# A hybrid encoder layer on one core: most of the values' products made in two row tiles of 64 contraction rows, each with its own bank, summed at the evacuation

## The chip, the core and the metric

The kernel runs on one NeuronCore of a Trainium2 chip. TensorE (PE) multiplies: it loads a stationary operand of up to 128x128 (a weight load, PEld in the profile) and streams a moving operand of up to 512 columns past it; the result goes to a bank of PSUM, of which there are eight, each 128 x 512 fp32. VectorE (DVE) and ScalarE (ACT) read PSUM and work on SBUF, GpSimd (POOL) works on SBUF alone, and SyncE (SP) issues most of the transfers between HBM and SBUF. Each engine works through its own queue in order; semaphores order the engines among each other.

The metric is device time in microseconds of one launch, the median of the runs. Lower is better.

## The reference

One layer is run (DEPTH is 1): an RMS norm, one projection to queries, keys, values and a gate, neighbourhood attention on a 32 x 64 grid of tokens, a SiLU gate, the output projection with its residual, and a final RMS norm. 2048 tokens, width 1024, 16 heads of 64.

```python
def neighbourhood_mixer(h, w_in, rpb):
    B, S, _ = h.shape
    proj = h @ w_in
    q, k, v, gate = jnp.split(proj, 4, axis=-1)
    heads = lambda a: a.reshape(B, S, N_HEADS, HEAD_DIM)
    o = neighbourhood_attention(heads(q), heads(k), heads(v), rpb)
    return o.reshape(B, S, D_INNER), gate
...
        h = rmsnorm(x, g)
...
            o, gate = neighbourhood_mixer(h, w_in, rpb)
...
        x = x + (o * jax.nn.silu(gate)) @ w_out
    return rmsnorm(x, norm_f)
```

The change touches the part of `h @ w_in` that makes the values v.

## The kernel before

All large products are made in rounded fp32 (the type F32R). To keep the precision, an operand is split into a high half `h` (ACT rounds it with a copy) and a low half `l` (DVE subtracts the high half from the operand). A product of two operands is three matmuls into one bank: high x high, high x low, low x high.

The contraction over the width of 1024 has eight steps `k` of 128 rows. Tokens are split into four blocks of 512, and a block into four tiles of 128.

*Values.* `values_of(X1, u, ts, ks)` (lines 549 to 560) makes the values of the token tiles `ts` for the unit `u` (512 columns of values; two units) over the steps `ks`. The stationary operand is 128 rows (the step) by 128 tokens of x, the moving one 128 rows by the 512 columns of the weights: an output of 128 tokens by 512 columns in one bank, named "pv". With eight steps and three matmuls each, a tile takes 24 matmuls. With 16 tiles and two units there are 768. After each, `due(1)` advances a count by which delayed work (stores above all) is issued.

`evac_v(u, t, p)` (line 389) takes a finished bank: ACT copies it with a scale to an SBUF tile `v`, and eight counts later SP stores that tile to a DRAM buffer `vd`. The weights of the values are split by `split_v` (line 532) into `W[u, b]`, a pair of tiles of two steps each, b = 0 to 3; ACT makes the high halves (line 539) and DVE the low ones (line 542). The four pairs fill the eight buffers of the pool `wp`, so the second unit's pair b can be written only once the first unit's pair b has been used for the last time.

*The rest of the projections.* Queries, keys and gate of tokens 0 to 1023 (stage one), and in part those of tokens 1024 to 2047 (stage two), are made by `seven_products` (line 402), with seven products in place of eight, line 435. Those left over are made during the attention (lines 379 to 383).

*Order.* Each engine's queue follows the order of the program, which is written out by hand. In stage one, unit 0's tiles come first: 0 to 3 together, 4 and 5, 6 and 7. Then come unit 1's tiles one by one through `tile_v` (line 757), in the order 4, 5, 6, 7, 0, 1, 2, 3, with other work handed in after each: the evacuation of the tile before, forms of x for the seven products, and twice `spread_rstd` (line 226), two full matmuls (lines 229 and 230) into a bank of its own that ACT copies (line 235). In stage two, `pair(u, ts, *do)` (line 831) goes through the four blocks of weights b, for each makes the products of the tiles `ts`, and then issues the piece `do[b]`. Unit 0's tiles 8 to 15 are made two at a time, unit 1's one at a time:

```python
        pair(0, (8, 9), both(w(0, 3), lambda: spread_rstd(3)), both(lw(1, 0), block("B12", x12, 0, 1)), block("B12", x12, 2, 3),
             block("B22", x22, 0, 1))
        pair(0, (10, 11), both(v(0, 8, 9), block("B22", x22, 2, 3)), t123(0), t123(1), lw(1, 1))
        pair(0, (12, 13), v(0, 10, 11), t123(2), t123(3), both(t4(0, 1, 2, 3), lw(1, 2)))
        pair(0, (14, 15), both(v(0, 12, 13), w(1, 0)), both(w(1, 1), lw(1, 3)), w(1, 2), w(1, 3))
```

Here `w(u, b)` splits a block of weights, `lw` loads one, `v` evacuates tiles, `block` scales and splits a block of x (lines 513, 517, 518), and `t123` and `t4` form differences of x on DVE (lines 862 to 870). Just before, the last seven products of stage one are evacuated: DVE adds (line 453), GpSimd scales (line 455), and for the gate ACT makes a tanh (line 359) and DVE a product (line 360).

*Banks.* Every bank comes from one pool of eight, in turn (`bank`, line 117): a new one waits until whoever read the bank eight allocations before has finished.

*Attention.* The scores (line 1027) and the transposes (line 1112) are plain fp32 and use row tiles already: the two heads of a pair lie on partitions 0 to 63 and 64 to 127 and write to separate banks. The products with the values (line 1134) use two column tiles of 64. A matmul of plain fp32 stands in the trace as two records, a transpose as one.

Of the kernel before, what the change touches and what calls it, by code (L numbers as in the profile page):

```python
# [14 lines left out]
AF = mybir.ActivationFunctionType  # L15
OP = mybir.AluOpType
# [5 lines left out]
NK = D // 128  # L22
# [48 lines left out]
def build(ctx, tc, x, xr, xt, wg, rpb, last, w_out, n0, nf, masks, out):  # L71
    nc = tc.nc
# [44 lines left out]
    def bank(n, name):  # L117
        return banks.tile([128, n], F32, name=name, tag="bank")
# [12 lines left out]
    rth = one.tile([128, 8], F32, name="rth")  # L131
# [125 lines left out]
    for n, (k, j, ph, c) in enumerate(halves):  # L257
        a = (KINDS[k] + j, ph)
# [66 lines left out]
    def store(key, lag, f):  # L325
        n = len(later)
        while n and later[n - 1][0] > clock[0] + lag:
            n -= 1
        later.insert(n, (clock[0] + lag, key, f))

    def due(n):
        clock[0] += n
        while later and later[0][0] <= clock[0]:
            later.pop(0)[2]()
# [53 lines left out]

    def evac_v(u, t, p):
        v = ev([128, 512], F32, "v")  # L390
        nc.scalar.activation(v, p, AF.Copy, scale=rth[:, t:t + 1] if t < 8 else 0.5)
        dst = vd[u].rearrange("h n d -> n h d")[t * 128:t * 128 + 128]
        written.add(("v", u, t))
        store(("v", u, t), 8, lambda: nc.sync.dma_start(dst, v.rearrange("p (h d) -> p h d", h=4)))
# [128 lines left out]
    VR, W = {}, {}  # L523
# [23 lines left out]
    ps = {}  # L547

    def values_of(X1, u, ts, ks):
        for t in ts:  # L550
            if ks[0] == 0:
                ps[t] = bank(512, "pv")
        for k in ks:
            x = X1["B%d%d" % (k // 4 + 1, ts[0] // 4 % 2 + 1)][k % 4]
            h, l = W[u, k // 2][0][:, k % 2], W[u, k // 2][1][:, k % 2]
            for m, (a, b) in enumerate(((x[0], h), (x[0], l), (x[1], h))):
                for t in ts:
                    o = slice(t % 4 * 128, t % 4 * 128 + 128)
                    nc.tensor.matmul(ps[t], a[:, o], b, start=k == 0 and m == 0, stop=k == NK - 1 and m == 2)  # L559
                    due(1)  # L560

    def place_of(slot_):
        return slot_[0]([128, slot_[1]], F32R, "t")[:, :512] if isinstance(slot_, tuple) else slot_

    X2 = {}
# [4 lines left out]
    def stage_one():  # L570
        us = [("k", j) for j in range(4)] + [(k, j) for j in range(4) for k in "qg"]
        X1 = {f: [(xs([128, 512], F32R, "h"), xs([128, 512], F32R, "l")) for _ in range(4)]
              for f in ("B12", "B11", "B21", "B22")}
# [120 lines left out]
        for k in range(NK):  # L694
            if k == 0:
                for h in range(2):
                    if h == 0:
                        split_v(0, 1, 0, (0,), nc.vector)
                    split_to(*(t[:, parts_[h]] for t in X1["B11"][0]), land["x11"][0][:, parts_[h]], gain("x11", 0))
                    if h == 0:  # L700
                        split_v(0, 0, 0, (0,), fresh=False)
                    values_of(X1, 0, (2 * h, 2 * h + 1), (0,))
                continue
            elif k == 1:
                split_v(0, 0, 0, (1,))
                split_v(0, 1, 0, (1,))
            elif k in (2, 3):
                split_v(0, 0, 1, (k - 2,))
                split_v(0, 1, 1, (k - 2,))
            elif k % 2 == 0:  # L710
                split_v(0, 0, k // 2)
                split_v(0, 1, k // 2)
            f = "x%d1" % (k // 4 + 1)
            split("B" + f[1:], land[f][k % 4], k % 4, f)
            values_of(X1, 0, (0, 1, 2, 3), (k,))
# [4 lines left out]
        for a, b in ((0, 0), (1, 0), (0, 1), (1, 1)):  # L720
            load_v0(1, a, b)
        values_of(X1, 0, (4, 5), range(4))
        for k in range(4):
            split("B22", land["x22"][k], k, "x22")
# [4 lines left out]
        for t in range(4):  # L729
            evac_v(0, t, ps[t])  # L730
# [4 lines left out]
        for b in range(4):  # L735
            values_of(X1, 0, (6, 7), (2 * b, 2 * b + 1))
            if b == 0:
                split_v(1, 0, 0)
                split_v(1, 1, 0)
                square_rows(*halves_of(1)[4:])  # L740
                stats(1)
                for t in (4, 5):
                    evac_v(0, t, ps[t])
            else:
                split_v(1, 0, b)
                split_v(1, 1, b)
        for k in range(4):
            y = ev([128, 512], F32, "y")
            a, b, c = land["x11"][k], land["x12"][k], land["x22"][k]
# [4 lines left out]
        for t in (6, 7):  # L754
            evac_v(0, t, ps[t])

        def tile_v(t, *do):
            values_of(X1, 1, (t,), range(NK))
            for f in do:
                f()  # L760

# [5 lines left out]
        def some(f, x, *ks):  # L767
            return lambda: [split(f, land[x][k], k) for k in ks]
# [4 lines left out]
        def t1(*ks):  # L773
            return lambda: [split("T1", land["x12"][k], k, "x11") for k in ks]

        v = lambda t: lambda: evac_v(1, t, ps[t])
        tile_v(4, some("T2", "x11", 0, 1, 2, 3))
        tile_v(5, v(4), t4, slot(-9), some("T3", "x22", 0, 1))
        tile_v(6, v(5), some("T3", "x22", 2, 3), slot(-8, -7))
        tile_v(7, v(6), lambda: diagonal(0), some("T4", "x21", 0), slot(-6))  # L780
        tile_v(0, v(7), lambda: spread_rstd(0), some("T4", "x21", 1), lambda: diagonal(1))
        tile_v(1, v(0), lambda: spread_rstd(1), t1(0, 1, 2))
        tile_v(2, v(1), t1(3), some("T4", "x21", 2, 3))
        values_of(X1, 1, (3,), (0, 1))
        v(2)()
        ahead(-5)
        values_of(X1, 1, (3,), (2, 3))
        ahead(-4)
        ahead(-3)
        values_of(X1, 1, (3,), (4, 5))  # L790
        ahead(-2)
        values_of(X1, 1, (3,), (6, 7))
        ahead(-1)
        v(3)()
        run()
# [2 lines left out]
    def stage_two():  # L798
# [30 lines left out]
        ahead, run = seven_products(units_two, 2, X2, also)  # L829

        def pair(u, ts, *do):
            for b in range(4):
                values_of(X2, u, ts, (2 * b, 2 * b + 1))
                if b < len(do):
                    do[b]()

        def both(*fs):
            return lambda: [f() for f in fs]
# [42 lines left out]
        def t1(*ks):  # L881
            def g():
# [3 lines left out]
            return g  # L886
# [6 lines that stand above are left out]
        pair(1, (12,), v(0, 14, 15), form("T2", x11, 0), form("T2", x11, 1))  # L893
# [530 lines left out]

    pair_steps = range(10, 24, 2)
    stage_one()
    stage_two()
    attending[0] = True
    for m in range(cycles + 1):
        a = amount[m] - 8  # L1430
# [111 lines left out]
```

## Time and profile before

| | |
|---|---|
| Time, median of 3 runs | 1057.04 us (1056.35 to 1057.21) |
| Span of the profiled execution | 1054.4 us |
| Busy: PE / PEld | 1046.1 us (99%) / 858.8 us (81%) |
| Busy: DVE / ACT / POOL | 696.7 us (66%) / 537.2 us (51%) / 252.0 us (24%) |
| Records of PE matmuls | 7316 |
| Chain that ended last: line 435 / line 559 | 36% / 17% |

The profile is of one execution, and of that the span from its first to its last instruction is given; its time with what lies around the span is not listed apart. Records are listed as start, duration, engine, line, operation, output<-inputs, tile (rows by columns of the stationary operand for PE) and shape; "x2" means that two records in sequence were merged, and the duration runs to the end of the second. A note in brackets gives the idle time of the engine before the record and what ended it. Groups are listed as shape, count, busy time (overlaps counted once) and mean duration in ns. PE's records overlap, since a matmul ends some time after the next one has started: the pace is read from starts.

### The profile page before, as it was taken

Reading aid. Unit: us, or ns where it says so; the run is one execution under the profiler, and the core shown is the slowest. Engines: PE = TensorE matmul, PEld = TensorE weight load, DVE = VectorE, ACT = ScalarE, POOL = GpSimd, SP = SyncE. Lnnn points to the kernel's source line nnn. Section 1 sums busy time; section 2 is a strip of 40 time slices with the busy share of each in tenths; the row PEclk is TensorE's granted clock in tenths of the full one; section 3 lists DMA queues with packets and bytes.
Section 4 is the critical chain, followed back from the end, with each engine's and each line's share of the span. In section 5 each row is a group of like instructions: output and inputs, shape, how many; then the busy total and the mean of one; then the engine's idle time right before and its main releaser. Section 6 shows DMA issues by size and latency. Waiting matters only on the chain.

```text
span 1054.4 us, 20160 instructions
## 1 busy us (share of the span) xinstructions
PE 1046.1 (99%) x7316; PEld 858.8 (81%) x7316; DVE 696.7 (66%) x1570; ACT 537.2 (51%) x1260; POOL 252.0 (24%) x342
## 2 busy tenths in 40 slices
PE   9999999999999999999999999999999999999997
PEld 7888888887888888888888788888887888888886
DVE  5476667778897625555655766687777886667554
ACT  7645223443444334232332677688787865455422
POOL 0000322312211000000002467666665322112100
PEclk9999999999999999999999999999999999999999
DMA  9634444343635433333236777778777588775352
GB/s 320 219 100 118 132 150 136 120 144 120 187 119 154 121 100 93 116 110 121 90 110 211 219 232 235 219 252 281 243 237 217 184 277 272 245 233 183 120 166 80
DMA packets 120252, 184.19 MB, mean 175 GB/s; under 512 B 10776, under 2 KB 55064, under 8 KB 120152
## 3 DMA queue, kind: packets, MB, share of 16 engines
q1 hardware_dynamic: 119720, 182.50, 55.1%
q8 instruction: 57, 0.93, 0.4%
q10 hardware_dynamic: 432, 0.40, 0.1%
q14 instruction: 43, 0.35, 0.1%
HBM read 132.53 MB, written 50.33 MB: 173 GB/s over the span
## 4 chain that ended last, share of the span: by engine, by line
PE 96%; DVE 2%; issue 1%; ACT 1%; DMA 0%; SPq 0%; DVEq 0%; ACTq 0%
PE pp L435 36%; PE pv L559 17%; PE s L1027 8%; PE o L1134 8%; PE po L1346 6%; PE po L1348 5%; PE po L1350 5%; PE ph L1112 4%; PE pp L381 2%; PE pp L383 2%; PE pp L379 2%; DVE f L418 0%; DVE x L1035 0%; DMA raw<-in_wg_dram 0%; DVE raw L424 0%
## 5 line engine op out<-in xcount | busy, mean ns | idle before, releaser
L435 PE MATMUL pp<-h,f 128*128 128x512 f32 x672 | 217.4, 389 | 0.0
L1041 ACT ACTIVATE x<-x,st 128x360 f32<-128x360 f32 (+5 forms) x256 | 151.1, 592 | 23.0 <-DVE st L1035 23.0
L1055 POOL TENSOR_SCALAR x<-x,st 128x480 f32<-128x480 f32 (+5 forms) x192 | 111.7, 599 | 153.5 <-DVE st L1046 148.6
L435 PEld LDWEIGHTS pp<-h,f 128*128 128x128 f32 x672 | 126.2, 188 | 26.2
L435 PE MATMUL pp<-t,f 128*128 128x512 f32 x558 | 141.7, 389 | 0.1
L435 PE MATMUL pp<-l,f 128*128 128x512 f32 x336 | 130.7, 389 | 0.0
L1035 DVE CUSTOM_DVE_ANT_0 x<-s,em 128x360 f32<-128x360 f32 (+5 forms) x256 | 123.0, 535 | 0.5 <-PE s L1027 0.4
L435 PEld LDWEIGHTS pp<-t,f 128*128 128x128 f32 x558 | 104.7, 188 | 22.2 <-DVE u L448 0.6
L455 POOL TENSOR_TENSOR tmp<-tmp,rb 128x512 f32<-128x512 f32 x36 | 58.4, 1622 | 268.3 <-DVE tmp L453 232.8
L995 POOL TENSOR_TENSOR em<-e,mk 128x264 f32<-128x264 f32 (+3 forms) x64 | 50.8, 825 | 259.8 <-PE pp L435 246.3
L418 DVE TENSOR_TENSOR f<-raw,f 128x512 fp32r<-128x512 f32 x105 | 76.5, 729 | 43.6 <-ACT f L417 43.5
L1346 PE MATMUL po<-woh,gh 128*128 128x512 f32 x252 | 99.8, 396 | 0.1
L1348 PE MATMUL po<-woh,gl 128*128 128x512 f32 x252 | 98.7, 391 | 0.0
L1350 PE MATMUL po<-wol,gh 128*128 128x512 f32 x252 | 98.6, 391 | 0.0
L1027 PE MATMUL s<-kt,q 64*128 64x480 f32 (+5 forms) x512 | 94.6, 487 | 0.0
L1134 PEld LDWEIGHTS o<-pta,vt 120*64 120x64 f32 (+2 forms) x1792 | 80.9, 137 | 13.9 <-DVE st L1035 13.6
L559 PE MATMUL pv<-wh,h 128*128 128x512 f32 x256 | 88.3, 390 | 0.0
L559 PE MATMUL pv<-wl,h 128*128 128x512 f32 x256 | 88.2, 390 | 0.2 <-DVE wl L542 0.2
L559 PE MATMUL pv<-wh,l 128*128 128x512 f32 x256 | 88.2, 389 | 0.0
L1088 DVE COPY pta<-ph 120x512 f32<-120x512 f32 (+5 forms) x96 | 56.9, 639 | 43.5 <-PE ph L1112 43.3
L1134 PE MATMUL o<-pta,vt 120*64 120x128 f32 (+5 forms) x1792 | 85.3, 253 | 0.0
L1027 PEld LDWEIGHTS s<-kt,q 64*128 64x128 f32 x512 | 64.9, 186 | 15.3 <-DVE pta L1088 1.3
(156 smaller groups left out, 1705.3 us busy)
## 6 DMA issues: line engine op xcount, KB each, us to landing
raw<-in_wg_dram SPq DMA_DIRECT2D x124, 256.0 KB, 4.3
row<-in_xr_dram SPq DMA_DIRECT2D x32, 256.0 KB, 4.1
vd<-v SPq DMA_DIRECT2D x32, 256.0 KB, 2.5
sgd<-sg SPq DMA_DIRECT2D x32, 256.0 KB, 2.4
q<-qd SPq DMA_DIRECT2D x32, 256.0 KB, 5.2
sgt<-sgd SPq DMA_DIRECT2D x32, 256.0 KB, 4.9
xr<-in_x_dram SPq DMA_DIRECT2D x32, 256.0 KB, 3.8
ogd<-og SPq DMA_DIRECT2D x32, 256.0 KB, 2.7
```

Of the source, the lines that this page charges most:

```text
L418: nc.vector.tensor_tensor(t[:, 1], src, t[:, 0].bitcast(F32), OP.subtract)
L435: nc.tensor.matmul(B[n, P], t[:, int(m == 2), c], x[k][int(m == 1)], start=P in (1, 6, 5) and k == 0 and m == 0, stop=k == 3 and m == 2, s ...
L455: nc.gpsimd.tensor_tensor(tmp, tmp, rb[c], OP.mult)
L559: nc.tensor.matmul(ps[t], a[:, o], b, start=k == 0 and m == 0, stop=k == NK - 1 and m == 2)
L1027: nc.tensor.matmul(pst[s], qt[a, qs], kt[a, :r1 - r0, c0:c1].rearrange("p r (s c) -> p s r c", c=8), start=True, stop=True)
L1035: nc.vector.tensor_tensor_reduce(X[i, C][s], pst[s], EM[p, ROW_TYPE[T], COL_TYPE[C], s], -1.0, 1e38, OP.add, OP.min, st[:, o:o + 1])
L1041: nc.scalar.activation(X[i, C][s], X[i, C][s], AF.Exp, bias=st[:, o:o + 1], scale=-1.0, accum_out=st[:, 4 + o:5 + o])
L1055: nc.gpsimd.tensor_scalar(X[i, C][s], X[i, C][s], st[:, o:o + 1], 1.0, op0=OP.mult, op1=OP.mult)
L1134: nc.tensor.matmul(to.rearrange("d (h q) -> d h q", q=64) if nq > 64 else to, vt[:k, strip, s * 64:s * 64 + 64], t[:k, h, at:at + 64] if n ...
L1346: nc.tensor.matmul(p, gh, woh[q, j], start=(i == 0), stop=False)
L1348: nc.tensor.matmul(p, gl, woh[q, j], start=False, stop=False)
L1350: nc.tensor.matmul(p, gh, wol[q, j], start=False, stop=(i == NK - 1))
```

## The change

The values' products of unit 1 in stage one and of both units in stage two go through a new function. It takes one token tile at a time, gives it two banks ("pv" and "pw"), and makes every matmul twice: once with rows 0 to 63 of both operands into the first bank, once with rows 64 to 127 into the second. `due(1)` is counted once for both. The evacuation copies the first bank with the scale, as before, and then DVE multiplies the second bank by the same scale and adds it to the tile. The stores take the tile after that.

In stage two a pair of tiles is no longer made block by block together: all four blocks of the first tile come first, then those of the second. The pieces handed in keep their numbers and are spread over both tiles, so that with two tiles a piece follows every second block.

Stage one's unit 0 stays with `values_of`.

```diff
     def evac_v(u, t, p):
         v = ev([128, 512], F32, "v")
-        nc.scalar.activation(v, p, AF.Copy, scale=rth[:, t:t + 1] if t < 8 else 0.5)
+        scale = rth[:, t:t + 1] if t < 8 else 0.5
+        nc.scalar.activation(v, p[0] if isinstance(p, tuple) else p, AF.Copy, scale=scale)
+        if isinstance(p, tuple):
+            nc.vector.scalar_tensor_tensor(v, p[1], scale, v, op0=OP.mult, op1=OP.add)
...
+    def values_halved(X1, u, t, ks):
+        if ks[0] == 0:
+            ps[t] = bank(512, "pv"), bank(512, "pw")
+        o = slice(t % 4 * 128, t % 4 * 128 + 128)
+        for k in ks:
+            x = X1["B%d%d" % (k // 4 + 1, t // 4 % 2 + 1)][k % 4]
+            h, l = W[u, k // 2][0][:, k % 2], W[u, k // 2][1][:, k % 2]
+            for m, (a, b) in enumerate(((x[0], h), (x[0], l), (x[1], h))):
+                for r in range(2):
+                    q = slice(64 * r, 64 * r + 64)
+                    nc.tensor.matmul(ps[t][r], a[q, o], b[q], start=k == 0 and m == 0, stop=k == NK - 1 and m == 2)
+                due(1)
...
         def tile_v(t, *do):
-            values_of(X1, 1, (t,), range(NK))
+            values_halved(X1, 1, t, range(NK))
...
-        values_of(X1, 1, (3,), (0, 1))
+        values_halved(X1, 1, 3, (0, 1))
         v(2)()
         ahead(-5)
-        values_of(X1, 1, (3,), (2, 3))
+        values_halved(X1, 1, 3, (2, 3))
...
         def pair(u, ts, *do):
-            for b in range(4):
-                values_of(X2, u, ts, (2 * b, 2 * b + 1))
-                if b < len(do):
-                    do[b]()
+            for n, t in enumerate(ts):
+                for b in range(4):
+                    values_halved(X2, u, t, (2 * b, 2 * b + 1))
+                    i = (4 * n + b) // len(ts)
+                    if (4 * n + b) % len(ts) == len(ts) - 1 and i < len(do):
+                        do[i]()
```

More of the change, by code (lines that the diff above doesn't have):

```diff
@@ L783, in stage_one @@
         tile_v(2, v(1), t1(3), some("T4", "x21", 2, 3))
-        values_of(X1, 1, (3,), (0, 1))
+        values_halved(X1, 1, 3, (0, 1))
         v(2)()
         ahead(-5)
-        values_of(X1, 1, (3,), (2, 3))
+        values_halved(X1, 1, 3, (2, 3))
         ahead(-4)
         ahead(-3)
-        values_of(X1, 1, (3,), (4, 5))
+        values_halved(X1, 1, 3, (4, 5))
         ahead(-2)
-        values_of(X1, 1, (3,), (6, 7))
+        values_halved(X1, 1, 3, (6, 7))
         ahead(-1)
```

## The prediction

> **What bounds the kernel now.** I read the page first (busy shares, the granted clock, the chain that ended last), then the busy time of each engine over the three stretches of the values' products that the change touches.
>
> ```profile
> span 1054.4 us, 20160 instructions
> PE   9999999999999999999999999999999999999997
> PEclk9999999999999999999999999999999999999999
> PE 96%; DVE 2%; issue 1%; ACT 1%; DMA 0%; SPq 0%; DVEq 0%; ACTq 0%
> core 0: us, PE busy (x) PEld busy (x) DVE busy (x) ACT busy (x) POOL busy (x), PEclk, DMA share, GB/s
> 48.30:93.30 45.00, 45.00 (x199) 37.18 (x198) 31.98 (x56) 25.62 (x45) 0.00 (x0) 1.00 0.37 101
> 323.10:367.40 44.30, 44.30 (x196) 36.63 (x196) 30.68 (x47) 14.80 (x26) 1.77 (x2) 1.00 0.45 124
> 367.40:410.70 43.30, 43.30 (x192) 35.86 (x191) 16.02 (x26) 17.39 (x33) 0.00 (x0) 1.00 0.32 92
> ```
>
> PE is the bound: 96% of the chain, full clock, and in the three stretches busy from edge to edge. So a change of the PE stream counts one for one; what DVE and ACT get counts only where PE must wait for it. How fast PE goes there is the distance between starts, not the length of a record, since records overlap:
>
> ```profile
> 379.67 0.39 PE L559 MATMUL pv<-wl,h 128*128 128x512 f32 x1
> ...
> 381.94 0.39 PE L559 MATMUL pv<-wh,l 128*128 128x512 f32 x1
> 379.90 0.19 PEld L559 LDWEIGHTS pv<-wh,h 128*128 128x128 f32 x1
> ```
>
> Ten steps take 2.27 us: one product of 128x512 every 0.227 us. The weight load of 0.19 us starts with a product (379.90) and is over before the next one starts, so it costs at most the small gap that is left between two streams.
>
> **The products (576 of them).** L559 makes 768 values' products; those of tiles 0 to 7 of unit 0 (192) stay, 8 tiles of unit 1 in stage one (192) and 16 tiles in stage two (384) are halved. Each becomes two, of 64 rows, with the same 512 columns. No work is saved: half the contraction rows stream as many columns. If the two tiles run side by side, a pair takes about what one product took; what a pair really takes no row shows, so I bound it.
>
> ```profile
> L1027 PE MATMUL s<-kt,q 64*128 64x480 f32 x128 | 30.9, 566 | 0.0
> L1134 PE MATMUL o<-pta,vt 120*64 120x128 f32 x512 | 38.9, 276 | 0.0
> L1134 PE MATMUL o<-pta,vt 120*64 120x64 f32 x384 | 21.9, 221 | 0.0
> ```
>
> The two L1134 rows differ by 55 ns over 64 columns: 0.86 ns a column for a pass of plain fp32. At that, the 128 records of the scores (L1027, two row tiles in two banks) would need 128 x 480 x 0.86 = 52.8 us one after the other; they are busy 30.9 us. So row tiles do run side by side here, in plain fp32. If a column of the rounded fp32 takes half as long as a plain one (an assumption), 512 columns stream in 220 ns, and 7 of the 227 ns are gap; the rows are rounded, and with a difference of 54 ns it would be 216 and 11. Lower end: the gap vanishes, 216 to 220 ns a pair, -7 to -11 ns. Upper end: nothing overlaps, 454 ns. Between them: the gap belongs to each tile (its own weights, its own stream) and stays: 227 ns, and some ns for the second start. I take 228, +1 ns a pair, 576 x 1 = +0.6 us, because the gap sits between a tile's own two streams, and a second tile with the same rhythm does not fill it. A higher price without serialising is the widest spacing of two full products in sequence:
>
> ```profile
> 325.88 0.40 PE L229 MATMUL prb<-dgh,onesr 128*128 128x512 f32 x1
> 326.12 0.40 PE L230 MATMUL prb<-dgl,onesr 128*128 128x512 f32 x1
> 326.36 0.63 PE L559 MATMUL pv<-wh,h 128*128 128x512 f32 x2
> ```
>
> 240 ns, +13 ns a pair. [...]
>
> **Changes between full and halved mode.** There are ten: into the halved tiles and out (2 in each stage), and around `spread_rstd` (4 in stage one, 2 in stage two).
>
> ```profile
> 660.64 0.39 PE L379 MATMUL pp<-h,w 128*128 128x512 f32 x1
> 660.96 0.42 PE L1112 MATMUL ph<-ident,x 64*88 64x64 f32 x8
> ```
>
> From a full product to the 64-row tiles 0.32 us pass instead of 0.227: 0.09 us. Taken for each way: +0.9 us (lower end 0.45, if the way back is free).
>
> **The order in stage two.** `pair(0,(8,9))` went through the four blocks of weights with both tiles; now tile 8 takes all four, then tile 9. The work handed in between keeps its place (after 12 products), but tile 8 needs the fourth block after 18 pairs, not after 36 products. Is it there?
>
> ```profile
> 323.15 0.62 PE L559 MATMUL pv<-wh,h 128*128 128x512 f32 x2
> 326.35 1.62 POOL L455 TENSOR_TENSOR tmp<-tmp,rb 128x512 f32<-128x512 f32 x1 [3.09 <-issue]
> 327.99 0.63 ACT L359 ACTIVATE sg<-tmp 128x512 f32<-128x512 f32 x1 [4.07 <-POOL tmp L455]
> 328.53 1.14 ACT L539 ACTIVATE wh<-raw 128x512 fp32r<-128x512 f32 x2
> 329.57 0.58 ACT L235 ACTIVATE rb<-prb 128x512 f32<-128x512 f32 x1
> 329.27 1.28 DVE L542 TENSOR_TENSOR wl<-raw,wh 128x512 fp32r<-128x512 f32 x2
> ```
>
> The two splits of block 3 stand on ACT behind the gate's tanh (L359), which waits for GpSimd: high half at 329.67, low half at 330.55, 6.5 and 7.4 us after the stage's first product at 323.15. Before, PE came there after 36 x 0.227 + 0.7 (spread) = 8.9 us, so nothing waited. Now it comes after 18 x 0.227 + 0.7 + 0.2 (two changes of mode) = 5.0 us: it waits 1.5 to 1.6 us for the high half, makes one pair, and waits another 0.65 us for the low half. **About +2.25 us**, on the path, as nothing else is in PE's queue. ACT's order is not touched, so the wait is not earlier work's doing.
>
> Next comes the bank. A tile takes two of eight banks in turn, `spread_rstd` one: tile 11's second bank is tile 8's first, which ACT frees:
>
> ```profile
> 341.51 0.63 ACT L517 ACTIVATE h<-land 128x512 fp32r<-128x512 f32 x1 [1.42 <-DVE land L513]
> 342.05 1.07 ACT L391 ACTIVATE v<-pv 128x512 f32<-128x512 f32 x2
> 342.53 0.59 ACT L391 ACTIVATE v<-pv 128x512 f32<-128x512 f32 x1
> ```
>
> The first evacuation ends at 342.6, 19.5 us after 323.15. PE comes to tile 11 at 72 x 0.228 + 0.7 + 0.3 + 2.25 = 19.6 us: no more wait. But a faster pair would only wait there: up to tile 11, this stretch cannot gain.
>
> Unit 0's weights are now let go by tile 15 (after 30, 36, 42, 48 pairs of the last pair), not by both tiles at once; unit 1's splits wait for that and are used 18 pairs (4.1 us) later each.
>
> ```profile
> 361.51 1.15 ACT L539 ACTIVATE wh<-raw 128x512 fp32r<-128x512 f32 x2 [1.56 <-PE pv L559]
> 362.17 1.29 DVE L542 TENSOR_TENSOR wl<-raw,wh 128x512 fp32r<-128x512 f32 x2 [1.43 <-ACT wh L539]
> ```
>
> One block takes 362.17 + 1.29 - 361.51 = 1.95 us of the 4.1: hidden, with 2.1 us to spare; later blocks come every 1.36 us and DVE needs 1.29. I cost it at nothing.
>
> **The sum at the evacuation.** 24 more DVE operations with one operand in PSUM.
>
> ```profile
> L448 DVE TENSOR_TENSOR u<-pp,p 128x512 f32<-128x512 f32 x42 | 28.9, 689 | 24.7 <-PE pp L435 24.7
> L391 ACT ACTIVATE v<-pv 128x512 f32<-128x512 f32 x16 | 9.1, 593 | 33.6 <-issue 18.0 <-PE pv L559 15.6
> ```
>
> At 0.69 us (the like of L448) that is 16.5 us of DVE, 5.5 in each of the three stretches, where it is idle 13.0, 13.6 and 27.3 us by the windows above. It covers them; were it full, each would cost 0.69 us. Each now waits on DVE for ACT's copy, and what stands behind it there (block B22's last two, `t123`) moves some 1.4 us per pair of tiles; tile 12 needs B22 only 9 us later. The stores on SP's queue wait for DVE instead of ACT, about 1 us longer, and the weight loads behind them are used over 10 us later. Cost: nothing.
>
> **Sum.** Products +0.6, mode +0.9, late weights +2.25: **+3.8 us**, against the profiled execution a span of 1058.2. That execution is told by its span of 1054.4; the median of the runs is 2.6 us above it, so 1057.0 + 3.8 = **1060.8 us**. Bounds of the unmeasured prices in this case: spacing 227 to 231 and mode 0.45 to 0.9 give +2.7 to +5.5, so 1059.7 to 1062.5.
>
> **Rivals.**
> *The gap closes* (the other side): place, the gap between two streams of the same tile; price g per pair. For it: L1027 shows that tiles overlap. Against it: no row shows a gap filled by the other tile. Only 504 pairs count (72 stand before tile 11's bank), and against them 2.5 us at tile 11 and 7 x 0.09 for mode: 3.1 - 0.504 g. It decides from g = 6.2 ns (220.8 a pair). At 220, -0.4: 1056.6. At 216, -2.4: 1054.6. [...] Faster by over 0.2% (2.1 us; less than that a measurement of this kernel cannot tell from no change) needs 10.3 ns, so about half of this case.
> *The tiles run one after the other*: rounded fp32 may use the array's whole input. For it: 30.9 us over 128 x 480 columns is 0.50 ns a column of both tiles together, no faster than the full product's 227/512 = 0.44; side by side the halves would need 0.22, which no row shows. Against it: plain fp32 overlaps. 576 x 0.227 = +130.8, mode +0.9, no wait for weights: 1188.7. In that case the change does not do what it says.
> *Dearer pairs*: 240 ns. 576 x 13.3 = 7.7, mode 0.9, weights 2.0 (PE comes 0.24 us later): +10.6, 1067.6.
>
> **Chances.** Gap stays (forecast) 0.40, gap closes 0.34, one after the other 0.15, dearer pairs 0.11. Range 1054.6 to 1067.6: it leaves out the serial case and the edges of the two others, a little under 0.2. The likeliest case's own range is 1059.7 to 1062.5. Faster: half of the closing gap, 0.17. Same: its other half and a sliver of the forecast, 0.19. Slower: 0.64.
>
> **What would show it.** The spacing of pairs in the middle of stage two (228 against 220 or less, 240, 454). A wait of PE of about 1.6 and 0.65 us some 5 us after stage two begins, put down to wh and wl. No wait, or a tenth, at tile 11 if pairs take 228; half a microsecond if they are faster. 0.09 us at each change of mode. The sums at 0.69 us, and no PE wait named after them. Wrong it would be if PE waits for a bank in stage one or at tiles 12 to 15, or if DVE's sums push out work that PE needs.

## The result, and the profile after

The changed kernel takes 1061.57 us (four runs, 1060.88 to 1062.33) against 1057.04: a ratio of 1.0046, 95% interval 1.0031 to 1.006. On another chip it took 1060.88 (1059.96 to 1062.12) against 1056.90, ratio 1.0040 (1.0027 to 1.0054). It is slower, by 4 to 4.5 us.

The page of the changed kernel, its span and its chain:

```profile
span 1059.7 us, 21345 instructions
PE 95%; DVE 2%; issue 1%; ACT 1%; POOL 0%; DVEq 0%; ACTq 0%
```

The bound is the same. The span is 5.3 us longer than before, and the time of every run lies 1.8 us above its span. Where the 5.3 us are is read from PE's timeline. Each matmul of line 575 stands twice, first bank (pv) and second bank (pw); columns are start, duration, engine, line.

In the middle of stage two:

```profile
356.48 0.39 PE L575 MATMUL pv<-wh,h 64*128 64x512 f32 x1
356.48 0.39 PE L575 MATMUL pw<-wh,h 64*128 64x512 f32 x1
...
357.16 0.39 PE L575 MATMUL pv<-wh,h 64*128 64x512 f32 x1
```

The two tiles of a pair start within the same hundredth of a microsecond, and three pairs take 0.68 us: 0.227 us a pair, what one full product took. The two tiles run fully side by side, and nothing is won or lost by it.

Around `spread_rstd` in stage two:

```profile
327.07 0.39 PE L575 MATMUL pv<-wh,l 64*128 64x512 f32 x1
...
327.39 0.50 PE L229 MATMUL prb<-dgh,onesr 128*128 128x512 f32 x1
327.73 0.39 PE L230 MATMUL prb<-dgl,onesr 128*128 128x512 f32 x1
328.04 0.49 PE L575 MATMUL pv<-wh,h 64*128 64x512 f32 x1
...
328.38 0.39 PE L575 MATMUL pv<-wl,h 64*128 64x512 f32 x1
...
328.61 0.39 PE L575 MATMUL pv<-wh,l 64*128 64x512 f32 x1
```

Five steps take 1.54 us; at 0.227 they would take 1.135. So two changes of mode cost 0.4 us, 0.2 each, and not only at the first product after the change (0.32 instead of 0.227) but also at the second (0.34 and 0.33). Ten changes are 1.9 to 2.0 us.

Some 5 us into stage two, at tile 8's fourth block of weights:

```profile
329.31 0.39 PE L575 MATMUL pv<-wh,l 64*128 64x512 f32 x1
...
330.90 0.50 PE L575 MATMUL pv<-wh,h 64*128 64x512 f32 x1 [1.20 <-ACT wh L542]
...
331.79 0.50 PE L575 MATMUL pv<-wl,h 64*128 64x512 f32 x1 [0.39 <-DVE wl L545]
...
332.13 0.40 PE L575 MATMUL pv<-wh,l 64*128 64x512 f32 x1
...
333.08 0.59 PE L575 MATMUL pv<-wh,h 64*128 64x512 f32 x1
...
333.89 0.63 PE L575 MATMUL pv<-wh,l 64*128 64x512 f32 x1
...
334.32 0.63 PE L575 MATMUL pv<-wh,h 64*128 64x512 f32 x1
...
336.72 0.39 PE L575 MATMUL pv<-wh,h 64*128 64x512 f32 x1
```

The steps to 330.90, 331.79 and 332.13 are 1.59, 0.89 and 0.34 us; with 0.227 taken off each, 2.1 us are lost, put down to the high and then the low half of the weights. (The bracket names less, because records overlap: the engine is idle only once the record before has ended.) The 0.34 has no wait beside it in the trace, and is as long as the late second product at the changes of mode (0.34 and 0.33). Then something comes that the prediction did not have: from 333.08 to 336.72 nine pairs take 3.64 us instead of 2.04, most of them 0.43 us each. The busy time by windows, with the granted clock ahead of the last two columns, says why:

```profile
331.50:333.00 1.50, 1.21 (x10) 1.02 (x12) 0.90 (x2) 0.57 (x1) 0.00 (x0) 1.00 0.99 214
333.00:336.60 3.60, 3.60 (x21) 2.84 (x20) 2.71 (x4) 0.76 (x3) 0.00 (x0) 0.53 0.51 122
336.60:340.00 3.40, 3.40 (x34) 2.77 (x32) 2.10 (x4) 1.20 (x2) 0.00 (x0) 1.00 0.00 0
```

Over 3.6 us after the wait the clock was granted at 0.53 on average; in windows of a quarter of a microsecond it is 0.50 for 3.4 us, from 333.1 to 336.5. That is 1.6 us lost. Waits 2.1, slow clock 1.6 and changes of mode 1.9 are 5.6 of the 5.3 us; the rest of the kernel came out 0.3 us shorter in this execution.

The sums on DVE, as groups (count, busy, mean in ns, idle before):

```profile
L394 DVE SCALAR_TENSOR_TENSOR v<-pw,v 128x512 f32<-128x512 f32 x16 | 10.7, 687 | 21.0 <-ACT v L392 21.0
L394 DVE SCALAR_TENSOR_TENSOR v<-pw,rth,v 128x512 f32<-128x512 f32 x8 | 6.0, 745 | 0.6 <-ACT v L392 0.6
```

They take 16.7 us of DVE, 0.69 to 0.75 us each, and in stage two DVE sits idle for 21 us in all just before them, until ACT's copy is done. PE waits nowhere after them.

### The profile page after: what moved, and what is told of

Same layout as the page of the kernel before. It is cut to its first block, busy times and chain, and to the rows that moved or that the text cites. A ratio compares the mean times of both kernels' runs of the same rounds, so it can differ in the third digit from the quotient of the medians.

```text
span 1059.7 us, 21345 instructions
## 1 busy us (share of the span) xinstructions
PE 1050.4 (99%) x7892; PEld 859.2 (81%) x7892; DVE 711.5 (67%) x1594; ACT 537.2 (51%) x1260; POOL 252.8 (24%) x342
## 4 chain that ended last, share of the span: by engine, by line
PE 95%; DVE 2%; issue 1%; ACT 1%; POOL 0%; DVEq 0%; ACTq 0%
PE pp L438 36%; PE pv L575 12%; PE s L1045 8%; PE o L1152 8%; PE po L1364 6%; PE po L1366 5%; PE po L1368 5%; PE pv L562 4%; PE ph L1130 4%; PE pp L381 2%; PE pp L383 2%; PE pp L379 2%; DVE f L421 0%; PE zp L124 0%; DVE x L1053 0%
## 5 line engine op out<-in xcount | busy, mean ns | idle before, releaser
L420 ACT ACTIVATE f<-raw 128x512 fp32r<-128x512 f32 x105 | 63.7, 624 | 26.5 <-PE pp L438 12.5
L575 PE MATMUL pv<-wh,h 64*128 64x512 f32 x192 | 75.6, 394 | 1.2 <-ACT wh L542 1.2
L575 PE MATMUL pw<-wh,h 64*128 64x512 f32 x192 | 75.6, 394 | 0.0
```

Source lines behind the costliest of these rows:

```text
L420: nc.scalar.activation(t[:, 0], src, AF.Copy)
L575: nc.tensor.matmul(ps[t][r], a[q, o], b[q], start=k == 0 and m == 0, stop=k == NK - 1 and m == 2)
```

## The experiments

**Tiles 8 and 9 by blocks again (e1).** Is it the order that lets the weights come late, and does a bank bind next?

```diff
         def pair(u, ts, *do):
+            if ts == (8, 9):
+                for b in range(4):
+                    for t in ts:
+                        values_halved(X2, u, t, (2 * b, 2 * b + 1))
+                    do[b]()
+                return
             for n, t in enumerate(ts):
```

> Tiles 8 and 9 go through the blocks of weights together again, halved, with four banks; all else as in the changed kernel. Theory (late weights, then the bank): the waits for wh and wl (1.4 and 0.7 us) go, but PE now comes to tile 11 some 17.7 us after stage two begins and its second bank is free at 19.5 us, so a wait of about 1.8 us appears there, named after ACT's evacuation, and the slow clock may follow it: time as changed or up to 1 us less, 1060.5 to 1061.6. Rival (the order alone is to blame, the bank never waits): 1058.5 to 1059.0, and no wait at tile 11.

Measured: 1058.19 us against 1056.83, ratio 1.0011 (1.0002 to 1.002); no step of PE in stage two longer than a change of mode. So the waits go with the order, as expected, and this trace has no slow clock either (1.00 from 330 to 342 us), but the wait at tile 11 that I expected does not come; the time is even below what the rival said. The first product of tile 11 on PE, and ACT's evacuation of tile 8:

```profile
342.30 0.39 PE L575 MATMUL pw<-wh,h 64*128 64x512 f32 x1
```

```profile
343.73 1.07 ACT L392 ACTIVATE v<-pv 128x512 f32<-128x512 f32 x2
```

Tile 11 writes to its second bank 1.4 us before ACT begins to read tile 8's. So it has another bank. In the program of the changed kernel as built, where each tile's bank is named, tile 11's second bank is the one that `spread_rstd` had, and tile 8's two go to tile 12; its first two products wait for an ACT and for a DVE instruction, the readers of those banks. So the pool does not hand out its banks strictly in turn, although the section on the kernel before says so: `spread_rstd`'s bank is let go earlier in the program than tile 8's, and it comes first. My count of the banks was wrong.

**The same with tiles 8 and 9 evacuated earlier (e2).**

```diff
-             block("B22", x22, 0, 1))
-        pair(0, (10, 11), both(v(0, 8, 9), block("B22", x22, 2, 3)), t123(0), t123(1), lw(1, 1))
+             both(v(0, 8, 9), block("B22", x22, 0, 1)))
+        pair(0, (10, 11), block("B22", x22, 2, 3), t123(0), t123(1), lw(1, 1))
```

> As the run before, and tiles 8 and 9 are evacuated one step earlier in the program, ahead of block B22's first two. Theory: neither the weights nor the bank is waited for and the clock stays at 1.0; only the changes of mode are left, ten at about 0.2 us: 1058.8 to 1059.1. Rival (halved pairs or DVE's sums cost something of their own in stage two): 1060 or more.

Measured: 1057.90 us against 1056.83, ratio 1.0011 (1.0003 to 1.002). The same as the run before it, and some 1 us less than I expected of the ten changes of mode; the interval (0.3 to 2.1 us) holds the 1.9 us of the trace. No bank is waited for in either, and halved pairs and sums cost nothing of their own in stage two.

**The order alone (e4).** Full products and one bank a tile, tile by tile:

```diff
-            for b in range(4):
-                values_of(X2, u, ts, (2 * b, 2 * b + 1))
-                if b < len(do):
-                    do[b]()
+            for n, t in enumerate(ts):
+                for b in range(4):
+                    values_of(X2, u, (t,), (2 * b, 2 * b + 1))
+                    i = (4 * n + b) // len(ts)
+                    if (4 * n + b) % len(ts) == len(ts) - 1 and i < len(do):
+                        do[i]()
```

> The kernel before with full products and one bank a tile, but stage two tile by tile as in the change. Theory (order): PE comes to the fourth block 0.3 us earlier than in the changed kernel, waits about 2.5 us and loses 1.6 us to the slow clock after it: 1057.0 + 4.1 = 1061.1. Rival (the two tiles, their banks or the sums are to blame): within 0.5 us of 1057.0.

Measured: 1059.96 us (1058.39 to 1060.52) against 1056.83, ratio 1.0027 (1.0017 to 1.0037): +3.1 us. Its timeline of PE at the same place:

```profile
327.62 0.40 PE L559 MATMUL pv<-wh,l 128*128 128x512 f32 x1
329.82 0.50 PE L559 MATMUL pv<-wh,h 128*128 128x512 f32 x1 [1.80 <-ACT wh L539]
330.71 0.79 PE L559 MATMUL pv<-wl,h 128*128 128x512 f32 x1 [0.39 <-DVE wl L542]
331.30 0.63 PE L559 MATMUL pv<-wh,l 128*128 128x512 f32 x1
331.73 0.63 PE L559 MATMUL pv<-wh,h 128*128 128x512 f32 x1
```

The waits are there with full products too (2.0 and 0.7 us), and products 0.43 us apart after them. Most of the change's loss is its order, not its tiles: 3.1 us with the order alone, 1.1 to 1.4 with halved tiles and the old order for tiles 8 and 9. It came out 1 us less than I expected.

**Filling the wait (e3, e9).** Is it the wait that lowers the clock? Eight pairs that nobody reads, put where PE would wait, into the banks that tile 9 overwrites afterwards (a second hunk, left out here, keeps tile 9 from taking banks of its own):

```diff
                 for b in range(4):
+                    if (u, t, b) == (0, 8, 3):
+                        ps[9] = bank(512, "pv"), bank(512, "pw")
+                        for i in range(8):
+                            for r in range(2):
+                                q = slice(64 * r, 64 * r + 64)
+                                nc.tensor.matmul(ps[9][r], X2["B11"][i % 4][0][q, :128], W[u, 0][0][q, 0], start=True, stop=True)
                     values_halved(X2, u, t, (2 * b, 2 * b + 1))
```

> The changed kernel with eight extra halved pairs (1.8 us of PE work whose result is overwritten) just before tile 8's fourth block, where PE would wait for wh. Theory (the wait lets the clock fall afterwards): the pairs at 427 ns are gone, the weights are waited for no longer than before, so the time falls by about 1.6 us to 1060.0 although PE does more. Rival (the slow pairs have another cause): the extra pairs are hidden or add up to 0.5 us, the slow pairs stay: 1061.6 to 1062.1.

The first try had no `u` in its condition, so the extra pairs came a second time in unit 1, where nothing waits: 1062.03 us (1061.70 to 1064.20) against 1056.83, ratio 1.0055 (1.0042 to 1.0068). It tells nothing of the time, but its trace has no pairs at 0.43 us in stage two. With the condition mended, and the changed kernel beside it:

> The changed kernel with the eight extra pairs before the fourth block of unit 0's tile 8 alone (the run e3_filler had them a second time, in unit 1, where PE does not wait, 1.8 us too much). Theory (the clock falls after the wait, in most executions): the extra pairs lie in the wait, the waits end no later, no pairs at 427 ns: about 1.0 to 1.6 us below the changed kernel run beside it. Rival (the clock has nothing to do with the wait): equal to the changed kernel or up to 0.5 us above it.

> The changed kernel once more, beside the filler on the same chip, to see in how many executions the slow pairs come. Theory: 1060.9 to 1062.3 as before, the lower ones without slow pairs (waits 2.1 us and changes of mode alone), the upper ones with them.

Measured: with the extra pairs 1059.98 us (1059.83 to 1060.46), the changed kernel 1060.88 (1059.96 to 1062.12), both against 1056.90. PE in the run with the extra pairs (line 855):

```profile
329.88 0.39 PE L855 MATMUL pv<-wh,h 64*128 64x512 f32 x1
...
331.71 0.39 PE L575 MATMUL pv<-wh,h 64*128 64x512 f32 x1
...
332.14 0.50 PE L575 MATMUL pv<-wl,h 64*128 64x512 f32 x1
...
332.48 0.40 PE L575 MATMUL pv<-wh,l 64*128 64x512 f32 x1
```

1.8 us of added work fit into the wait, and the low half is met at the same moment as before (7.4 us after stage two begins in both). The median is 0.9 us lower, but the ranges overlap. The profiled execution of the changed kernel run beside it had the same waits and this window:

```profile
331.49 0.50 PE L575 MATMUL pv<-wh,h 64*128 64x512 f32 x1 [1.20 <-ACT wh L542]
...
332.38 0.50 PE L575 MATMUL pv<-wl,h 64*128 64x512 f32 x1 [0.39 <-DVE wl L545]
```

```profile
333.00:336.60 3.60, 3.60 (x35) 2.95 (x32) 2.21 (x4) 1.27 (x2) 0.00 (x0) 1.00 0.65 139
```

Clock 1.00, and no slow pairs. So the clock falls after this wait in some executions and not in others. Six traces have the two waits in full (1.4 or 2.0 us, then 0.7 us): three of them show the slow stretch (the changed kernel, e4, and e8 below), three do not (this one, e5 and e6 below). The other six, those of before, e1, e2, e3, e7 and e9, have neither the waits in full nor a slow stretch while PE multiplies. In e4 and e8 the stretch reads:

```profile
330.20:333.80 3.60, 3.21 (x9) 2.47 (x9) 2.48 (x4) 1.07 (x3) 0.00 (x0) 0.53 0.80 167
```

```profile
325.90:329.50 3.60, 3.60 (x20) 2.83 (x18) 2.21 (x4) 1.26 (x2) 0.00 (x0) 0.53 0.79 134
```

That the filler prevents the fall is not shown. Its two traces have no slow pairs, but at three in six that would happen by chance one time in four. And its lower median need not come from the clock: the two profiled executions, both without slow pairs, took 1060.39 us with the extra pairs and 1060.62 us without.

**Without the sums (e5).** The DVE operation of line 394 is left out, and with it half of the contraction.

```diff
-        if isinstance(p, tuple):
-            nc.vector.scalar_tensor_tensor(v, p[1], scale, v, op0=OP.mult, op1=OP.add)
```

> The changed kernel without DVE's sums: the second bank is never read, so half of the contraction of these values is left out. Theory (the 24 sums are covered): within 0.4 us of the changed kernel. Rival (they delay something that PE needs): faster by up to 16.5 us, at least 1 us.

Measured: 1061.88 us (1060.72 to 1062.26) against 1056.57, ratio 1.0050 (1.0036 to 1.0063). Without the sums the kernel is no faster than with them (1.0046 and 1.0040 above), so they are covered.

**More changes of mode (e6).** One step of eight in full products:

```diff
+                if k == 4:
+                    nc.tensor.matmul(ps[t][0], a[:, o], b, start=False, stop=False)
-                for r in range(2):
+                for r in range(2) if k != 4 else ():
```

> The changed kernel, but in each of the 24 halved tiles one step of eight (k = 4) is made with full products into the first bank: 48 more changes of mode, the same streaming. By the price that the changed kernel's trace shows (0.09 us at the first product and about 0.1 at the second, each way): +9.4 us on the changed kernel, 1071. By the price of the prediction (0.09 each way): +4.3, 1066. If a change of mode costs nothing: 1061.6.

Measured: 1070.80 us against 1056.57, ratio 1.0135 (1.0122 to 1.0149). One of the changes, out to the full products and back:

```profile
58.26 0.39 PE L577 MATMUL pv<-wh,l 64*128 64x512 f32 x1
...
58.58 0.50 PE L574 MATMUL pv<-wh,h 128*128 128x512 f32 x1
58.92 0.40 PE L574 MATMUL pv<-wl,h 128*128 128x512 f32 x1
59.15 0.40 PE L574 MATMUL pv<-wh,l 128*128 128x512 f32 x1
59.48 0.50 PE L577 MATMUL pv<-wh,h 64*128 64x512 f32 x1
...
59.81 0.39 PE L577 MATMUL pv<-wl,h 64*128 64x512 f32 x1
```

That is 14.2 us above before, against 4.5 for the changed kernel: 9.7 us for 48 changes, 0.20 each. The price of two late products for a change stands (the expectation of 9.4), not that of one (4.3).

**What the gap is (e7, e8).** Unit 1's tiles in stage one are cut to fewer columns after their first step, full and halved; the other columns are not computed.

```diff
                     q = slice(64 * r, 64 * r + 64)
-                    nc.tensor.matmul(ps[t][r], a[q, o], b[q], start=k == 0 and m == 0, stop=k == NK - 1 and m == 2)
+                    w = {4: 512, 5: 448, 6: 384, 7: 320, 0: 256, 1: 288, 2: 352, 3: 480}[t] if u == 1 and t < 8 and k else 512
+                    nc.tensor.matmul(ps[t][r][:, :w], a[q, o], b[q, :w], start=k == 0 and m == 0, stop=k == NK - 1 and m == 2)
```

This is the halved version (e8); the full one (e7) cuts the one product in the same way.

> The kernel before, with the eight full tiles of unit 1 in stage one cut to 512, 448, 384, 320, 256, 288, 352 and 480 columns after their first step (the columns beyond are not computed). Read is the spacing of products against the width. A gap that belongs to each stream: 0.4167 ns a column and 13.5 ns more at every width (173.5 at 384, 120 at 256). A stream that is slower throughout: 0.443 ns a column and no constant (170 at 384, 113 at 256). [...]

> The changed kernel with the same cut of unit 1's eight tiles in stage one, halved. Read is the spacing of pairs against the width. If the gap is each tile's own: the same spacing as the full product at every width. If the second tile fills some of it where the stream is narrower: less than the full product there.

At 320 columns, full products and then halved ones:

```profile
66.23 0.31 PE L560 MATMUL pv<-wh,l 128*128 128x320 f32 x1
...
67.11 0.31 PE L560 MATMUL pv<-wh,l 128*128 128x320 f32 x1
```

```profile
66.25 0.31 PE L576 MATMUL pv<-wl,h 64*128 64x320 f32 x1
...
66.98 0.31 PE L576 MATMUL pv<-wh,h 64*128 64x320 f32 x1
```

Six full steps take 0.88 us, five halved ones 0.73: 0.147 us both. From 512 to 320 columns the spacing falls by 80 ns in 192 columns, 0.417 ns a column, so some 13 ns are no streaming: 0.147 - 320 x 0.000417 = 0.013. By that price of a column the other widths leave 12 to 14 ns from 256 to 384 columns, but 16 at 448 (203 ns apart) and 17 at 480 (217); why these two are dearer, no run tells. At every width the halved pairs have the full products' spacing to within 1 ns. So the gap hardly depends on the width, and the halved tiles have it just as the full ones. (Times, one run each: 1048.69 and 1055.43 us with the columns left out; the second has the late weights and the slow stretch as well.)

## Why the prediction was right, step by step

The time lay within 1 us of the forecast, 1060.8 against 1061.57, and the case that was forecast is the one that came: pairs at the spacing of a full product, a price for each change of mode, late weights. One term was too small (the changes of mode), two were too large (the pairs, and the late weights by a little), and one was missing (the slow clock). The errors cancel in part, so that the time came this close is partly luck.

- *Pairs.* +1 ns taken, 0 measured. That a second tile leaves the gap as it is, e7 and e8 show. My rows had put the gap at 7 ns (11 at most); it is 13 to 14 at 512 columns, because half of plain fp32's time per column (0.43 ns) overstates the rounded type's (0.417). The three rivals about the pair (gap closes, one after the other, 240 ns) are out with 0.227 us. The evidence that kept the serial case alive, that no two tiles together outran one full product, came from plain fp32 alone and said nothing of the rounded type.
- *Changes of mode.* Mis-sized: "From a full product to the 64-row tiles 0.32 us pass instead of 0.227: 0.09 us." The second product after each change is late as well, by another 0.1 us. 1.9 us by the trace, not 0.9; e6 confirms 0.2 each. The row that the price came from led into transposes, where a second 512-column product could not be seen.
- *Late weights.* +2.25 predicted, 2.1 measured, with both halves in the order and at the place foreseen. e1 takes it away by giving the old order back to two tiles, e4 makes it with nothing but the order.
- *The slow clock.* Missing. I followed the wait to its end and not to what PE does afterwards; up to 1.6 us, in three of the six traces with the waits.
- *The bank at tile 11.* No wait came, as forecast, but the reason was wrong: "tile 11's second bank is tile 8's first" falls with e1. The rival that let the gap close carried 2.5 us for it that it would not have paid.
- *Sums and the release of unit 0's weights.* Nothing, as predicted (e5 for the sums, and no PE step in the trace for either).
- *The frame.* The median of before lay 2.6 us above the span of its profile. What lies around a span is 1.8 us in the runs after it, so that profiled execution was one of the faster ones. The sum stood on the median, so this does not move it.

By the numbers as they turned out: 1057.0 + 1.9 + 2.1 = 1061.0 without the slow clock, 1062.6 with it, and the median of 1061.57 between. On the other chip the same sum gives 1060.9 without the slow clock, and the median was 1060.88.

No version here beats the kernel before: the halved pairs only equalled the full products (0.227 us both), and each change of mode took 0.2 us more.

## What to carry to other kernels

The scores, whose contraction fills 64 rows, were busy 30.9 us in two row tiles, against 52.8 one after the other (an estimate: 128 records of 480 columns at 0.86 ns). Cutting a full contraction in two kept the same stream and the same gap here (0.227 us a pair and a product, 13 to 14 ns of it gap), and added 0.2 us for each change between the modes. When a loop nest is reordered for the sake of banks, look up for each operand when it was ready and when it is now needed: here that cost more than the edit the change was named after. And a wait on PE may cost more than its length: after 2.1 us of waiting the changed kernel lost 1.6 us more at a clock of 0.50, and three of six traces with the waits have such a stretch, though that the wait is its cause is not shown.

## What was not expected of the hardware

After a wait of 1.4 us (2.0 in e4) and one of 0.7 us, with one step between them, the clock was granted at 0.50 in three of six traces. In each of the three it stayed there for 3.4 us (0.53 on average over 3.6 us). It began 1.3 us after the second wait in the changed kernel, 0.4 us after it in e8, and 0.5 us before its end in e4. That the waits bring it about is argued from this count and is not shown: the two traces with the wait filled are too few for it. Why the same waits are followed by it in one execution and not in the next, no run here tells.

At that clock pairs came 0.427 us apart, 0.83 ns a column, twice the 0.417 of the full clock: at 512 columns the constant gap of 13 ns is gone there. Why, no run here tells.
